# A hybrid decoder layer with sparse experts: one-hots of a gate table built eight tokens at a time, gather steps and last chunks in another order

## The chip, the cores and the metric

The kernel runs on one core of one Trainium2 chip. The metric is the device time of one execution in microseconds (us); of several runs the median is taken. The profile is of one further execution, with its own time.

## The reference, cut to what matters

The layer is attention and a gated recurrence side by side, then PEER: each of 512 tokens picks, for each of 8 heads, 16 of 16384 experts, and an expert is one row of `u` and one row of `v` (1024 numbers each). `h` is the normalised token, `idx` the 128 experts of a token, `gates` their softmax weights.

```python
def expert_block(args):
    ht, it, gt = args
    ue = jnp.take(u, it, axis=0)
    act = jax.nn.gelu(jnp.einsum('tkd,td->tk', ue, ht), approximate=False)
    ve = jnp.take(v, it, axis=0)
    return jnp.einsum('tk,tkd->td', gt * act, ve)
...
x = x + peer_layer(rms_norm(x, norm_ffn_g), w_peer_q, peer_keys, peer_u, peer_v)
...
return rms_norm(x, norm_final_g)
```

An expert's number is i1*128 + i2, from two lists of 128 keys. The inputs are float32.

## The kernel before, in words

**Two ways through the experts.** The first 160 tokens are done as the reference does them. 320 steps each fetch one expert row per partition by an indirect DMA (`gather`, L704, issued on POOL at L707, 512 KB, into one of four buffers `ga`), and then VectorE (DVE) uses the 128 rows: `sparse` (L711) multiplies them with `h` and sums (L715) or adds them, weighted, to the sum (L725). `pace(goal, after)` (L729) brings the number of gathers issued up to `goal`; behind each it records the DVE step of the gather three places earlier (`GLAG`), and that step may not stand on its engine ahead of the instruction `after`.

The other 352 tokens meet all experts as dense matrices. `u` comes in 128 chunks of 128 experts, each loaded by SP (L152), split into a high part `hi` by ScalarE (ACT, L142) and a rest `lo` by DVE (L162), and put through 24 matmuls (`act_pieces`, L638, matmuls L646: 16 with `hi`, then 8 with `lo`); ACT's Gelu (L652) leaves a tile `gel`. Three raw buffers (`S4`) and two each of `hi` and `lo` (`HB`) are turned over. Chunks of `v` are handled in the main loop.

**The gate table.** A gate of a token belongs to an expert (i1, i2). For each token TensorE multiplies a one-hot of i2 over the 128 picks by a one-hot of i1 that carries the gates, high and low part (two matmuls 128x128 in f16, L912). VectorE makes the one-hots for eight tokens at a time (`oh`, two buffers) by four operations, L904 to L907; `iok` is a table of the numbers 0 to 127, repeated. ACT copies four tokens' results from PSUM into `G` (L914), and each 16 tokens a DMA on ACT's queue stores `G` to the DRAM tensor `Gd` (L916): 22 steps. Between the one-hot matmuls `piece` (L672) feeds six matmuls of a U chunk at a time, 88 pieces in all, the matmuls kept in program order (`keep_in_program_order`). `pace((s_ + 1) // 3, ...)` sets gathers beside the table.

**Behind the table.** 26 U chunks are done ahead of the table and 22 in it; five more are held back (`HELD`): three by `fill` (L662) at once and two (`LASTU`) behind `g_load(0)`, which reads the first gates back from `Gd` (L936) and so waits for the last store. `pace(EARLY, ...)` brings the gathers to 16. In the text A is the chunk in work as the table ends, B, C, D the next three, E and F the last two.

**The main loop.** For each of 128 chunks of `v`: split (L142, L162), `w` = gel * gates (L980, waits for `gt`), its split (L142, L985), then 18 matmuls 128x512 (L994 to L996) into six PSUM banks `acc`; then U chunks still to do, then `pace` in proportion, with all gathers issued `TAILC` = 2 chunks before the end. The last two chunks (`TL`) go together. Behind the loop stand the last gather steps and `final_rows` (L960 add, L967 scale, store).

Within an engine a scheduler puts instructions in the order of the program unless an instruction's inputs are late by its reckoning; `tc.issue_after(x)` makes what is recorded under it stand behind `x` on their engine. Each queue (SP, ACT, POOL) issues its DMAs in order.

Of the kernel before, what the change touches and what calls it, by code (L numbers as in the profile page):

```python
# [17 lines left out]
P = 128  # L18
# [8 lines left out]
NE = 128  # L27
# [10 lines left out]
GS = 4096.0  # L38
GC = 4
TG = 16  # L40
QT = 4
OT = 8
LOOK = 26
LATE = 17
S4 = 3
# [1 line left out]
VPRE = 2  # L47
GLAG = 3
GB = 4
TAILC = 2  # L50
HELD = 5
LASTU = 2
EARLY = 16
# [63 lines left out]
def layer(nc, tc, a, out, probe=None, upto=99):  # L117
# [5 lines left out]
    cur = {}  # L123
# [31 lines left out]
    def wsplit(raw, shape, parts=1, eng=None):  # L155
        hi = oc.tile(list(shape), F32R, tag="hi", bufs=HB, name=nm("hi"))
        lo = oc.tile(list(shape), F32R, tag="lo", bufs=HB, name=nm("lo"))
        n = shape[1] // parts
        for i in range(parts):
            m = slice(i * n, (i + 1) * n)  # L160
            hi_of(hi[:, m], raw[:, m])
            (eng or V).tensor_tensor(lo[:, m], raw[:, m], hi[:, m].bitcast(F32), op=OP.subtract)  # L162
        return hi, lo


# [26 lines left out]
    with tc.tile_pool(name="front", bufs=1) as fr, tc.tile_pool(name="psf", bufs=1, space=PSUM) as psf:  # L192
# [79 lines left out]


        ktm, logf = [], []
        POOL.dma_start(gm, a["gmix"])
        POOL.dma_start(ones, a["const"][:, 5 * P:6 * P])
        ld = exp_ln_set()
        fb = proj_tm(0)
# [342 lines left out]
    with tc.tile_pool(name="peer", bufs=1) as pp, tc.tile_pool(name="psp", bufs=1, space=PSUM) as psp, ExitStack() as ps:  # L621
# [45 lines left out]
                    nu[0] += 1  # L667


        work = []  # L670

        def piece(limit):  # L672
            while len(work) < 2 and nu[0] < limit:
                work.append(act_pieces(next(todo), True))
                next(work[-1])
                nu[0] += 1
            if work and next(work[0], 0) == 0:
                work.pop(0)

        gta = pp.tile([P, NB, PH * TK], F32, name="gta")  # L680
# [195 lines left out]
        with tc.tile_pool(name="gb", bufs=1, reuse_waits="tile") as gp:  # L876
            iT = gp.tile([P, 2, DT], F16, name="iT")
            gs = gp.tile([P, DT], F32, name="gs")
            g16 = gp.tile([P, 2, DT], F16, name="g16")
            fill(2)  # L880
            for n in range(1, NB):
                f = X if n == 1 else 0
                t = slice((n - 1) * P - X + f, n * P - X)
                b = bank((P, 4, P))
                for w in range(2):
                    PE.transpose(b[:, w, :], i12[:, w, n, :], ident)
                PE.transpose(b[:, 2, :], gta[:, n, :], ident)
                ACT.activation(iT[:, :, t], b[:, 0:2, f:], AF.Copy)
                ACT.activation(gs[:, t], b[:, 2, f:], AF.Copy, scale=GS)  # L889
                V.tensor_copy(g16[:, 0, t], gs[:, t])  # L890
                V.tensor_tensor(g16[:, 1, t], gs[:, t], g16[:, 0, t], op=OP.subtract)
            NQ = OT // QT
            shape = [P, NQ, P, QT]
            for s_ in range(NPT):
                G_ = gp.tile([P, NE, TG], F32, tag="G", bufs=2, name=nm("G"))
                for o in range(TG // OT):
                    t = slice(s_ * TG + o * OT, s_ * TG + (o + 1) * OT)

                    def row(x):
                        return x.rearrange("p (q t) -> p q t", t=QT).unsqueeze(2).to_broadcast(shape)  # L900

                    ioq = iok.unsqueeze(1).to_broadcast(shape)
                    oh = gp.tile([P, 3, NQ, P, QT], F16, tag="oh", bufs=2, name=nm("oh"))
                    V.tensor_tensor(oh[:, 0], ioq, row(iT[:, 0, t]), op=OP.is_equal)  # L904
                    V.tensor_tensor(oh[:, 2], ioq, row(iT[:, 1, t]), op=OP.is_equal)
                    V.tensor_tensor(oh[:, 1], oh[:, 2], row(g16[:, 0, t]), op=OP.mult)
                    last = V.tensor_tensor(oh[:, 2], oh[:, 2], row(g16[:, 1, t]), op=OP.mult)  # L907
                    for q in range(NQ):
                        b = bank((P, QT, P))
                        for i in range(QT):  # L910
                            for w in range(2):
                                lastg = tc.keep_in_program_order(PE.matmul(b[:, i, :], oh[:, 0, q, :, i], oh[:, 1 + w, q, :, i], start=w == 0, stop=w == 1))  # L912
                        m = o * OT + q * QT
                        ACT.activation(G_[:, :, m:m + QT].rearrange("p c t -> p t c"), b, AF.Copy)  # L914
                        piece(KEEP - HELD)
                ACT.dma_start(Gd.rearrange("g p s f -> s p g f")[s_], G_.rearrange("p (g c) t -> p g (c t)", c=GC))  # L916
                pace((s_ + 1) // 3, last.ins)
        late = ps.enter_context(tc.tile_pool(name="late", bufs=1, reuse_waits="tile"))
        cur["late"] = late

# [12 lines left out]
        def g_load(g):  # L933
            if g < NE // GC:
                gts[g] = late.tile([P, NPT, GC * TG], F32, tag="gt", bufs=2, name=nm("gt"))
                return SP.dma_start(gts[g], Gd[g])  # L936

        with tc.issue_after(lastg.ins):
            fill(KEEP - nu[0] - LASTU)
        for c in range(VPRE):  # L940
            v_load(c)
        g0 = g_load(0)
        pace(EARLY, last.ins)
        with tc.issue_after(lastg.ins), tc.issue_after(g0.ins):
            fill(LASTU)

# [26 lines left out]
        for c in range(NE):  # L973
            if c % GC == 0:
                g_load(c // GC + 1)
            gtile = gts[c // GC][:, :, (c % GC) * TG:(c % GC + 1) * TG]
            v_load(c + VPRE)
            vh, vl = wsplit(vraw.pop(c), [P, D])
            w = late.tile([P, DT], F32, tag="w", bufs=2, name=nm("w"))
            V.scalar_tensor_tensor(w.rearrange("p (s t) -> p s t", t=TG), gel.pop(c).rearrange("p (s t) -> p s t", t=TG),  # L980
                                   1.0 / GS, gtile, op0=OP.mult, op1=OP.mult)
            whi = late.tile([P, DT], F32R, tag="whi", bufs=2, name=nm("whi"))
            hi_of(whi, w)
            wlo = late.tile([P, DT], F32R, tag="wlo", bufs=2, name=nm("wlo"))
            last = V.tensor_tensor(wlo, w, whi.bitcast(F32), op=OP.subtract)  # L985
            ready.append((c, whi, wlo, vh, vl))
            if c < NE - TL or c == NE - 1:
                for tb in range(DB):
                    t = slice(tb * P, min(tb * P + P, DT))
                    m = t.stop - t.start  # L990
                    for i, whi, wlo, vh, vl in ready:
                        for hf in range(2):
                            d = slice(hf * 512, (hf + 1) * 512)
                            PE.matmul(acc[tb][hf][0:m, :], whi[:, t], vh[:, d], start=i == 0, stop=False)  # L994
                            PE.matmul(acc[tb][hf][0:m, :], whi[:, t], vl[:, d], start=False, stop=False)  # L995
                            PE.matmul(acc[tb][hf][0:m, :], wlo[:, t], vh[:, d], start=False, stop=i == NE - 1)  # L996
# [24 lines left out]
            pace(EARLY + (NS - EARLY) * share, last.ins)  # L1021

        while nsp[0] < NS:
            sparse(nsp[0])
            nsp[0] += 1
        final_rows(ys[0], [sp0.ax[:, 0:512], sp0.ax[:, 512:]], 0, P)
        for n in range(DB):
            m = min(P, DT - n * P)
            final_rows(ys[n + 1][0:m, :], [acc[n][hf][0:m, :] for hf in range(2)], T0 + n * P, m)
# [17 lines left out]
```

## Time and profile before

| what | us |
|---|---|
| three runs: median (lowest to highest) | 1666.84 (1663.52 to 1667.65) |
| the profiled execution, its own time | 1675.46 |
| its span | 1673.7 |
| TensorE (PE) busy | 1605.2 (96 %) |
| VectorE (DVE) busy | 1321.9 (79 %) |
| ScalarE (ACT) busy | 709.6 (42 %) |
| GpSimd (POOL) busy | 487.3 (29 %) |
| mean granted TensorE clock | 0.986 of full |

The span is what the trace covers; the execution's own time is 1.8 us longer. In the timelines a row of several equal instructions gives the start of the first and the length from there to the end of the last; TensorE's matmuls overlap their neighbours, so the step from one start to the next, not the length, is what one costs. A wait is the idle time of an engine, with the instruction or the transfer that ended it.

### The profile page before, as it was taken

The numbers are of one execution on the slowest core, as the hardware profiler recorded it, in microseconds if no ns is written. First come the engines' busy times: TensorE is split into PE (matmuls) and PEld (weight loads), VectorE is DVE, ScalarE is ACT, GpSimd is POOL, SyncE is SP. The second block draws the span as 40 slices with busy tenths as digits, with TensorE's granted clock in tenths as the row PEclk, the third lists the DMA queues.
The fourth block names the chain that finished last, engine by engine and source line by source line (L and its number), as shares of the span: only waits on it lengthen the run. The fifth ranks groups of instructions, "written<-read, shape, count | busy, mean of one in ns | idle before, by whom it ended". The sixth has DMA issues, their size and how long they took to land.

```text
span 1673.7 us, 23435 instructions
## 1 busy us (share of the span) xinstructions
PE 1605.2 (96%) x8511; PEld 1358.7 (81%) x8511; DVE 1321.9 (79%) x2560; ACT 709.6 (42%) x1152; POOL 487.3 (29%) x341
## 2 busy tenths in 40 slices
PE   8999999999999969997899999999999999999996
PEld 6877678888988869997788888887888888888874
DVE  8456663647999988887688888878888888888887
ACT  5433353234554547775333333333333333333333
POOL 4000000000000010002455555445455555554542
PEclk9999999999999979999899999999999999999998
DMA  5311133334333347888999999999999999999984
GB/s 173 101 51 51 51 104 111 103 115 154 108 109 116 103 126 192 219 224 265 336 340 353 349 368 349 337 341 339 344 368 351 359 354 347 360 358 363 343 305 145
DMA packets 197491, 400.87 MB, mean 240 GB/s; under 512 B 103344, under 2 KB 105904, under 8 KB 197376
## 3 DMA queue, kind: packets, MB, share of 16 engines
q1 hardware_dynamic: 58832, 206.02, 35.2%
q0 software_dynamic: 46336, 168.39, 27.0%
q10 hardware_dynamic: 92208, 24.98, 6.1%
q8 instruction: 66, 1.08, 0.3%
q14 instruction: 49, 0.40, 0.1%
HBM read 371.91 MB, written 27.39 MB: 239 GB/s over the span
## 4 chain that ended last, share of the span: by engine, by line
PE 53%; issue 16%; POOL 12%; DVE 12%; DMA 6%; ACT 1%; POOLq 0%; DVEq 0%; SPq 0%; ACTq 0%
PE b L646 13%; POOL ga L707 11%; PE b L263 5%; PE b L262 5%; PE b L995 5%; PE b L996 5%; PE b L265 4%; PE b L994 4%; DMA ga<-v,idx 4%; PE b L912 4%; DVE lo L162 3%; DMA ga<-un,idx 1%; DVE ti L858 1%; DVE mr L856 1%; DVE e L725 1%
## 5 line engine op out<-in xcount | busy, mean ns | idle before, releaser
L707 POOL DMA_INDIRECT ga<-un,idx x160 | 225.2, 1407 | 944.5 <-ACT gs L889 581.3
L646 PE MATMUL b<-hT,hi 128*128 128x352 f32 x2048 | 366.9, 327 | 2.2 <-ACT hi L142 1.7
L646 PEld LDWEIGHTS b<-hT,hi 128*128 128x128 f32 x2048 | 334.4, 190 | 12.7 <-ACT hi L142 2.0
L995 PE MATMUL b<-lo,whi 128*128 128x512 f32 (+1 forms) x768 | 305.0, 397 | 15.0 <-DVE lo L162 14.6
L996 PE MATMUL b<-hi,wlo 128*128 128x512 f32 (+1 forms) x768 | 304.3, 396 | 0.0
L994 PE MATMUL b<-hi,whi 128*128 128x512 f32 (+1 forms) x768 | 302.7, 395 | 0.0
L707 POOL DMA_INDIRECT ga<-v,idx x160 | 240.4, 1502 | 208.3 <-DVE e L725 190.3
L142 ACT ACTIVATE hi<-s 128x1024 fp32r<-128x1024 f32 (+1 forms) x195 | 205.1, 1052 | 203.1 <-PE b L646 88.1
L162 DVE TENSOR_TENSOR lo<-s,hi 128x1024 fp32r<-128x1024 f32 (+1 forms) x195 | 238.5, 1224 | 29.7 <-ACT hi L142 28.0
L142 ACT ACTIVATE whi<-w 128x352 fp32r<-128x352 f32 x128 | 63.7, 498 | 400.0 <-PE b L995 361.2
L725 DVE SCALAR_TENSOR_TENSOR e<-ga,wt,e 128x1024 f32<-128x1024 f32 x158 | 202.2, 1280 | 19.3 <-DMA ga<-v,idx 18.4
L715 DVE SCALAR_TENSOR_TENSOR ga<-ga,h 128x1024 f32<-128x1024 f32 x160 | 194.5, 1220 | 28.6 <-DMA ga<-un,idx 26.9
L646 PE MATMUL b<-hT,lo 128*128 128x352 f32 x1024 | 191.3, 325 | 11.8 <-DVE lo L162 11.8
L995 PEld LDWEIGHTS b<-lo,whi 128*128 128x128 f32 (+1 forms) x768 | 138.8, 181 | 59.2 <-DVE lo L162 22.0
L646 PEld LDWEIGHTS b<-hT,lo 128*128 128x128 f32 x1024 | 168.0, 189 | 12.4 <-DVE lo L162 12.3
L996 PEld LDWEIGHTS b<-hi,wlo 128*128 128x128 f32 (+1 forms) x768 | 138.5, 180 | 39.3
L994 PEld LDWEIGHTS b<-hi,whi 128*128 128x128 f32 (+1 forms) x768 | 138.2, 180 | 35.3 <-ACT hi L142 1.2
L142 ACT ACTIVATE hi<-vr 128x1024 fp32r<-128x1024 f32 x128 | 134.6, 1051 | 75.9 <-PE b L646 46.3
L162 DVE TENSOR_TENSOR lo<-vr,hi 128x1024 fp32r<-128x1024 f32 x128 | 156.1, 1220 | 9.4 <-ACT hi L142 9.4
L263 PE MATMUL b<-hT,hi 128*128 128x512 f32 (+1 forms) x376 | 146.4, 391 | 0.3 <-DVE hT L145 0.3
L262 PE MATMUL b<-hT,hi 128*128 128x512 f32 (+1 forms) x376 | 146.1, 390 | 0.2
L985 DVE TENSOR_TENSOR wlo<-w,whi 128x352 fp32r<-128x352 f32 x128 | 67.0, 523 | 80.9 <-ACT whi L142 77.5
(284 smaller groups left out, 1960.5 us busy)
## 6 DMA issues: line engine op xcount, KB each, us to landing
s<-uc SPq DMA_DIRECT2D x128, 512.0 KB
vr<-vc SPq DMA_DIRECT2D x128, 512.0 KB
Gd<-G ACTq DMA_DIRECT2D x22, 1024.0 KB
gt<-Gd SPq DMA_DIRECT2D x32, 704.0 KB
s<-wfm SPq DMA_DIRECT2D x30, 512.0 KB
s<-wq SPq DMA_DIRECT2D x16, 512.0 KB
s<-wmg SPq DMA_DIRECT2D x8, 512.0 KB
s<-wout SPq DMA_DIRECT2D x8, 512.0 KB
```

The lines of the kernel that those rows point to most:

```text
L142: ACT.activation(dst, src, AF.Copy)
L162: (eng or V).tensor_tensor(lo[:, m], raw[:, m], hi[:, m].bitcast(F32), op=OP.subtract)
L262: PE.matmul(b, wh[:, k, :], rh(i), start=start and i == 0, stop=False)
L263: PE.matmul(b, wh[:, k, :], rl(i), start=False, stop=False)
L646: m = PE.matmul(o, w[:, k, :], z[:, k, t], start=i == 0, stop=i == 3 * KD - 1)
L707: tc.keep_in_program_order(POOL.indirect_dma_start(out=t, out_offset=None, in_=a[src], in_offset=bass.IndirectOffsetOnAxis(ap=b.idx[:, j:j ...
L715: V.scalar_tensor_tensor(t, t, 1.0, h20, op0=OP.mult, op1=OP.mult, accum_out=b.act[:, j:j + 1])
L725: V.scalar_tensor_tensor(b.ax, t, b.wt[:, j:j + 1], b.ax, op0=OP.mult, op1=OP.add)
L985: last = V.tensor_tensor(wlo, w, whi.bitcast(F32), op=OP.subtract)
L994: PE.matmul(acc[tb][hf][0:m, :], whi[:, t], vh[:, d], start=i == 0, stop=False)
L995: PE.matmul(acc[tb][hf][0:m, :], whi[:, t], vl[:, d], start=False, stop=False)
L996: PE.matmul(acc[tb][hf][0:m, :], wlo[:, t], vh[:, d], start=False, stop=i == NE - 1)
```

## The change

1. The one-hots of eight tokens are made by two DVE operations of 128x2048 in place of four of 128x1024. The layout of `oh` changes with it: a token's 128 values stand eight f16 apart (16 bytes) where they stood four apart (8 bytes); `iok` has 1024 entries in place of 512. The number and the order of the matmuls and of ACT's copies stay.
2. `piece` takes a second limit: loads and splits of two more U chunks are begun within the table, their matmuls left for after it. Each of the three chunks behind the table is followed by one gather, whose DVE step stands behind that chunk's `lo`; `pace(EARLY, ...)` goes behind the last of these.
3. Beside the table `pace` asks for a gather every two steps, 11 by its end, in place of 7.
4. `TAILC` is 5; the last gather steps and the first 128 tokens' `final_rows` stand in chunk 125 of the loop; the matmuls of the last two chunks run through the bank's halves ahead of the chunks.
5. `gm`, a load at the program's start, moves from POOL's queue to ACT's.

```diff
-QT = 4
-OT = 8
+QT = 8
+BT = 4
-TAILC = 2
+TAILC = 5
...
-        POOL.dma_start(gm, a["gmix"])
+        ACT.dma_start(gm, a["gmix"])
...
-        def piece(limit):
-            while len(work) < 2 and nu[0] < limit:
-                work.append(act_pieces(next(todo), True))
-                next(work[-1])
+        def piece(limit, ahead):
+            while len(work) < 2 and nu[0] < ahead:
+                c = next(todo)
+                work.append((c, act_pieces(c, True)))
+                next(work[-1][1])
                 nu[0] += 1
-            if work and next(work[0], 0) == 0:
+            if work and work[0][0] < limit and next(work[0][1], 0) == 0:
                 work.pop(0)
...
-                    oh = gp.tile([P, 3, NQ, P, QT], F16, tag="oh", bufs=2, name=nm("oh"))
-                    V.tensor_tensor(oh[:, 0], ioq, row(iT[:, 0, t]), op=OP.is_equal)
-                    V.tensor_tensor(oh[:, 2], ioq, row(iT[:, 1, t]), op=OP.is_equal)
-                    V.tensor_tensor(oh[:, 1], oh[:, 2], row(g16[:, 0, t]), op=OP.mult)
-                    last = V.tensor_tensor(oh[:, 2], oh[:, 2], row(g16[:, 1, t]), op=OP.mult)
+                    oh = gp.tile([P, 3, P, QT], F16, tag="oh", bufs=2, name=nm("oh"))
+                    V.tensor_tensor(oh[:, 1:3], ioq, iT[:, :, t].unsqueeze(2).to_broadcast(shape), op=OP.is_equal)
+                    last = V.tensor_tensor(oh[:, 0:2], oh[:, 1:2].to_broadcast(shape),
+                                           g16[:, :, t].unsqueeze(2).to_broadcast(shape), op=OP.mult)
...
-                                lastg = tc.keep_in_program_order(PE.matmul(b[:, i, :], oh[:, 0, q, :, i], oh[:, 1 + w, q, :, i], start=w == 0, stop=w == 1))
+                                lastg = tc.keep_in_program_order(PE.matmul(
+                                    b[:, i, :], oh[:, 2, :, q * BT + i], oh[:, 1 - w, :, q * BT + i],
+                                    start=w == 0, stop=w == 1))
...
-                        piece(KEEP - HELD)
+                        piece(KEEP - HELD, KEEP - HELD + 2)
...
-                pace((s_ + 1) // 3, last.ins)
+                pace((s_ + 1) // 2, last.ins)
...
+        held = cur["lo"]
+        for c_, g_ in work:
+            for _ in g_:
+                pass
+            pace(nga[0] + 1, held.ins)
         with tc.issue_after(lastg.ins):
-            fill(KEEP - nu[0] - LASTU)
+            for _ in range(KEEP - nu[0] - LASTU):
+                fill(1)
+                held = cur["lo"]
+                pace(nga[0] + 1, held.ins)
...
-        pace(EARLY, last.ins)
+        pace(EARLY, held.ins)
...
-                    for i, whi, wlo, vh, vl in ready:
-                        for hf in range(2):
-                            d = slice(hf * 512, (hf + 1) * 512)
+                    for hf in range(2):
+                        d = slice(hf * 512, (hf + 1) * 512)
+                        for i, whi, wlo, vh, vl in ready:
...
-        while nsp[0] < NS:
-            sparse(nsp[0])
-            nsp[0] += 1
-        final_rows(ys[0], [sp0.ax[:, 0:512], sp0.ax[:, 512:]], 0, P)
+            if c == NE - 3:
+                while nsp[0] < NS:
+                    sparse(nsp[0])
+                    nsp[0] += 1
+                final_rows(ys[0], [sp0.ax[:, 0:512], sp0.ax[:, 512:]], 0, P)
```

The order of VectorE behind the table, before: the last one-hots (`oh`), then gather steps (`ga`, L715) and the `lo` parts of U chunks (L162), then the first `w`, which waits for the gates `gt`.

```order
L907 TENSOR_TENSOR oh_7456<-oh_7456,g_5521 128x1024
L715 SCALAR_TENSOR_TENSOR ga_6902,act_3079<-ga_6902,h_62 128x1024
L715 SCALAR_TENSOR_TENSOR ga_7159,act_3079<-ga_7159,h_62 128x1024
L715 SCALAR_TENSOR_TENSOR ga_7414,act_3079<-ga_7414,h_62 128x1024
L162 TENSOR_TENSOR lo_7349<-s_1252_7346,hi_7348 128x1024
L715 SCALAR_TENSOR_TENSOR ga_7609,act_3079<-ga_7609,h_62 128x1024
L715 SCALAR_TENSOR_TENSOR ga_7612,act_3079<-ga_7612,h_62 128x1024
L715 SCALAR_TENSOR_TENSOR ga_7615,act_3079<-ga_7615,h_62 128x1024
L715 SCALAR_TENSOR_TENSOR ga_7618,act_3079<-ga_7618,h_62 128x1024
L715 SCALAR_TENSOR_TENSOR ga_7621,act_3079<-ga_7621,h_62 128x1024
L715 SCALAR_TENSOR_TENSOR ga_7624,act_3079<-ga_7624,h_62 128x1024
L162 TENSOR_TENSOR lo_7510<-s_1275_7507,hi_7509 128x1024
```

And now (the same lines are L903, L717 and L162):

```order
L903 TENSOR_TENSOR oh_7385<-oh_7385,g_5521 128x2048
L717 SCALAR_TENSOR_TENSOR ga_6932,act_3079<-ga_6932,h_62 128x1024
L162 TENSOR_TENSOR lo_7279<-s_1256_7276,hi_7278 128x1024
L162 TENSOR_TENSOR lo_7359<-s_1267_7356,hi_7358 128x1024
L717 SCALAR_TENSOR_TENSOR ga_7096,act_3079<-ga_7096,h_62 128x1024
L162 TENSOR_TENSOR lo_7469<-s_1284_7466,hi_7468 128x1024
L717 SCALAR_TENSOR_TENSOR ga_7259,act_3079<-ga_7259,h_62 128x1024
L162 TENSOR_TENSOR lo_7504<-s_1289_7501,hi_7503 128x1024
L717 SCALAR_TENSOR_TENSOR ga_7422,act_3079<-ga_7422,h_62 128x1024
L717 SCALAR_TENSOR_TENSOR ga_7463,act_3079<-ga_7463,h_62 128x1024
L717 SCALAR_TENSOR_TENSOR ga_7498,act_3079<-ga_7498,h_62 128x1024
L988 SCALAR_TENSOR_TENSOR w_7620<-gel_3136,gt_7540 128x352
```

Between the last one-hots and the `lo` of chunk B stood nine gather steps and now stands one; the `lo` of C and D have one more each ahead of them, and three gather steps stand between D's `lo` and the first `w`.

VectorE in the tail of the changed kernel, from the last but one gather step (L727) on; `lo_14811` is the split of `v` chunk 124, `lo_14841` that of chunk 125:

```order
L727 SCALAR_TENSOR_TENSOR e_528_3077<-ga_14723,wt_3080,e_528_3077 128x1024
L727 SCALAR_TENSOR_TENSOR e_528_3077<-ga_14775,wt_3080,e_528_3077 128x1024
L968 TENSOR_TENSOR s_2731_14681<-s_2731_14681,b_14756 32x512
L968 TENSOR_TENSOR s_2731_14681<-s_2731_14681,b_14758 32x512
L162 TENSOR_TENSOR lo_14811<-vr_14726,hi_14810 128x1024
...
L968 TENSOR_TENSOR e_2729_14678<-e_2729_14678,e_528_3077 128x512
L162 TENSOR_TENSOR lo_14841<-vr_14778,hi_14840 128x1024
```

Before, the last gather step stood between the `lo` of chunk 126 and that of chunk 127, and the adds of the first 128 tokens behind both. Now it stands ahead of the `lo` of chunk 124.

## Rows read from the trace of the kernel before

**Rows 1.** Stretches: us; busy PE, PEld, DVE, ACT, POOL; granted clock, DMA share, GB/s

```profile
621.00:783.00 162.00, 160.72 (x1171) 148.68 (x1170) 140.10 (x200) 114.08 (x124) 10.40 (x7) 1.00 0.79 213
783.00:802.00 19.00, 6.53 (x34) 5.95 (x33) 8.44 (x13) 4.49 (x5) 8.53 (x7) 0.79 1.02 341
...
819.00:1640.00 821.00, 810.05 (x4039) 686.65 (x4039) 697.16 (x893) 297.07 (x408) 427.72 (x304) 1.00 0.95 348
1640.00:1674.00 34.00, 19.07 (x71) 13.66 (x69) 22.23 (x34) 10.73 (x29) 9.70 (x1) 0.81 0.34 115
```

**Rows 2.** Waits of PE, 819 to 1640: us in total, times, longest

```profile
PE b L995 <- DVE lo L162: 10.5, 12, 3.2
```

**Rows 3.** PE timeline, end of table: start us, length us, [idle before <-releaser]

```profile
775.31 1.11 PE L912 MATMUL b<-oh 128*128 128x128 f16 x8
776.17 1.22 PE L646 MATMUL b<-hT,hi 128*128 128x352 f32 x6
777.23 1.11 PE L912 MATMUL b<-oh 128*128 128x128 f16 x8
...
781.92 0.59 PE L646 MATMUL b<-hT,lo 128*128 128x352 f32 x2 [1.01 <-DVE lo L162]
...
799.72 2.71 PE L646 MATMUL b<-hT,lo 128*128 128x352 f32 x8 [10.75 <-DVE lo L162]
802.23 3.71 PE L646 MATMUL b<-hT,hi 128*128 128x352 f32 x16
...
818.82 0.40 PE L994 MATMUL b<-hi,whi 128*128 128x512 f32 x1
```

**Rows 4.** Waits of DVE, 775 to 805, as rows 2

```profile
DVE ga L715 <- DMA ga<-un,idx: 9.2, 4, 3.7
```

**Rows 5.** DVE timeline behind the table, as rows 3

```profile
798.44 2.35 DVE L162 TENSOR_TENSOR lo<-s,hi 128x1024 fp32r<-128x1024 f32 x2
...
808.26 0.96 DVE L980 SCALAR_TENSOR_TENSOR w<-gel,gt 128x352 f32<-128x352 f32 x2 [4.51 <-DMA gt<-Gd]
```

**Rows 6.** Waits of the queue of SP, 775 to 830, as rows 2

```profile
SPq L936 <- DMA Gd<-G: 20.4, 1, 20.4
```

**Rows 7.** ACT timeline behind the table, as rows 3

```profile
810.00 1.05 ACT L142 ACTIVATE hi<-s 128x1024 fp32r<-128x1024 f32 x1
```

**Rows 8.** Gathers (L707) from 1600 on: duration ns min/median/max, first and last start

```profile
L707 POOL DMA_INDIRECT ga<-v,idx x13: 936/1674/9908, 1600.6 to 1639.8; - x13
```

**Rows 9.** DVE timeline in the tail, as rows 3

```profile
1653.36 1.28 DVE L725 SCALAR_TENSOR_TENSOR e<-ga,wt,e 128x1024 f32<-128x1024 f32 x1 [4.48 <-DMA ga<-v,idx]
...
1663.06 2.73 DVE L967 SCALAR_TENSOR_TENSOR e<-e,rs,h 128x512 f32<-128x512 f32 x4
```

**Rows 10.** PE timeline in the tail, as rows 3

```profile
1655.84 0.80 PE L995 MATMUL b<-lo,whi 128*128 128x512 f32 x1 [4.04 <-DVE lo L162]
...
1662.71 0.40 PE L996 MATMUL b<-hi,wlo 128*96 128x512 f32 x1
```

**Rows 11.** Timeline of all engines at the start, as rows 3

```profile
5.31 0.72 ACT L216 ACTIVATE hT<-s,gm 128x512 fp32r<-128x512 f32 x1 [3.29 <-DMA gm<-gmix]
```

**Rows 12.** DVE groups by form: out<-in, shapes, count, busy us, mean ns, idle

```profile
L904 DVE TENSOR_TENSOR oh<-iok,iT 128x1024 f16<-128x1024 f16 x44 | 30.4, 691 | 23.1 <-PE b L912 22.2 <-ACT iT L888 0.8
...
L816 DVE TENSOR_TENSOR eq<-iota,r 128x2048 f16<-128x2048 f16 x8 | 9.8, 1224 | 0.7
```

**Rows 13.** PE groups by form, as rows 12

```profile
L646 PE MATMUL b<-hT,hi 128*128 128x352 f32 x2048 | 366.9, 327 | 2.2 <-ACT hi L142 1.7 <-ACT s L613 0.5
...
L912 PE MATMUL b<-oh 128*128 128x128 f16 x704 | 98.2, 296 | 3.2 <-DVE oh L906 2.0 <-DVE oh L907 1.2
...
L262 PE MATMUL b<-hT,hi 128*128 128x256 f32 x16 | 4.1, 294 | 0.1
```

**Rows 14.** ACT groups by form, as rows 12

```profile
L914 ACT ACTIVATE G<-b 128x512 f32<-128x512 f32 x88 | 96.0, 1091 | 54.3 <-PE b L912 50.7 <-issue 3.7
...
L844 ACT ACTIVATE qp<-b 128x512 f32<-128x512 f32 x15 | 9.0, 600 | 4.0 <-PE b L265 4.0
```

More of the change, by code (lines that the diff above doesn't have):

```diff
@@ L161, in wsplit @@
             hi_of(hi[:, m], raw[:, m])
-            (eng or V).tensor_tensor(lo[:, m], raw[:, m], hi[:, m].bitcast(F32), op=OP.subtract)
+            cur["lo"] = (eng or V).tensor_tensor(lo[:, m], raw[:, m], hi[:, m].bitcast(F32), op=OP.subtract)
         return hi, lo
@@ L885, in layer @@
                 for w in range(2):
-                    PE.transpose(b[:, w, :], i12[:, w, n, :], ident)
+                    PE.transpose(b[:, w, :], i12[:, 1 - w, n, :], ident)
                 PE.transpose(b[:, 2, :], gta[:, n, :], ident)
@@ L889, in layer @@
                 ACT.activation(gs[:, t], b[:, 2, f:], AF.Copy, scale=GS)
[L890 to L893, printed above, removed]
+                V.tensor_copy(g16[:, 1, t], gs[:, t])
+                V.tensor_tensor(g16[:, 0, t], gs[:, t], g16[:, 1, t], op=OP.subtract)
+            shape = [P, 2, P, QT]
+            ioq = iok.unsqueeze(1).to_broadcast(shape)
@@ L894, in layer @@
             for s_ in range(NPT):
                 G_ = gp.tile([P, NE, TG], F32, tag="G", bufs=2, name=nm("G"))
[L896 to L902, printed above, removed]
-                    oh = gp.tile([P, 3, NQ, P, QT], F16, tag="oh", bufs=2, name=nm("oh"))
-                    V.tensor_tensor(oh[:, 0], ioq, row(iT[:, 0, t]), op=OP.is_equal)
-                    V.tensor_tensor(oh[:, 2], ioq, row(iT[:, 1, t]), op=OP.is_equal)
-                    V.tensor_tensor(oh[:, 1], oh[:, 2], row(g16[:, 0, t]), op=OP.mult)
-                    last = V.tensor_tensor(oh[:, 2], oh[:, 2], row(g16[:, 1, t]), op=OP.mult)
-                    for q in range(NQ):
-                        b = bank((P, QT, P))
-                        for i in range(QT):
-                            for w in range(2):
-                                lastg = tc.keep_in_program_order(PE.matmul(b[:, i, :], oh[:, 0, q, :, i], oh[:, 1 + w, q, :, i], start=w == 0, stop=w == 1))
-                        m = o * OT + q * QT
-                        ACT.activation(G_[:, :, m:m + QT].rearrange("p c t -> p t c"), b, AF.Copy)
-                        piece(KEEP - HELD)
@@ new lines, in layer @@
+                for o in range(TG // QT):
+                    t = slice(s_ * TG + o * QT, s_ * TG + (o + 1) * QT)
+                    oh = gp.tile([P, 3, P, QT], F16, tag="oh", bufs=2, name=nm("oh"))
+                    V.tensor_tensor(oh[:, 1:3], ioq, iT[:, :, t].unsqueeze(2).to_broadcast(shape), op=OP.is_equal)
+                    last = V.tensor_tensor(oh[:, 0:2], oh[:, 1:2].to_broadcast(shape),
+                                           g16[:, :, t].unsqueeze(2).to_broadcast(shape), op=OP.mult)
+                    for q in range(QT // BT):
+                        b = bank((P, BT, P))
+                        for i in range(BT):
+                            for w in range(2):
+                                lastg = tc.keep_in_program_order(PE.matmul(
+                                    b[:, i, :], oh[:, 2, :, q * BT + i], oh[:, 1 - w, :, q * BT + i],
+                                    start=w == 0, stop=w == 1))
+                        m = o * QT + q * BT
+                        ACT.activation(G_[:, :, m:m + BT].rearrange("p c t -> p t c"), b, AF.Copy)
+                        piece(KEEP - HELD, KEEP - HELD + 2)
```

## The prediction

> **What bounds the kernel now.** I read first the table of stretches [rows 1]. While the gate table is built (621 to 783) TensorE is busy 160.72 of 162 us and VectorE 140.10: TensorE sets the pace. In the main loop it is busy 810.05 of 821 us, and of its waits there the view of waits names 10.5 us, for VectorE's `lo` [rows 2]. Two stretches are not full: 783 to 802, with 6.53 us of work in 19, and the tail from 1640, with 19.07 in 34. Only there can an order give much; in the other two only a dearer or cheaper matmul counts.
>
> Then the timeline of TensorE at the table's end [rows 3]. It stalls 1.01 us before 781.92 and 10.75 us before 799.72, both times for a `lo`. After the long stall it is slow as well: eight matmuls take 799.72 to 802.23, 2.51 us, where six took 777.23 less 776.17, 1.06, so eight should take 1.41; the next sixteen cover 3.71 us. The granted clock, full in the table, was 0.79 of full over that stretch [rows 1]. I put the slow matmuls at 2 us.
>
> Why the `lo` is late: VectorE waits 9.2 us in four gather steps, the longest 3.7 [rows 4], and makes the two `lo` only from 798.44 on [rows 5]. The order printed above says why: nine gather steps stand between the last one-hots and the second `lo`. But a second chain ends late too. SP's queue waits 20.4 us for the last store of the table before it may issue the load of the gates [rows 6]; VectorE's first `w` starts at 808.26, ended by that load [rows 5]; ACT splits chunk E only at 810.00, behind the two splits of `w` [rows 7]; so the main loop opens at 818.82 [rows 3].
>
> In the tail the last gather takes 9.91 us on POOL, the median of 13 being 1.674 [rows 8]. VectorE waits 4.48 us for it, until 1653.36 [rows 9], and TensorE 4.04 us behind that, until 1655.84; its last matmul starts at 1662.71 [rows 10]. From 1663.06 four operations of 2.73 us, of rows long complete, stand on VectorE ahead of the last add [rows 9].
>
> **The change, part by part.**
>
> *Behind the table.* The `lo` of A, B, C and D now have one gather step or none ahead of each. The stall of 1.01 goes. TensorE then has A's rest and B, C, D, three chunks of 24 matmuls at 1.06/6 = 0.177, 4.2 us each: work until about 797. What is late next is the gates. The store is in line with gathers: before, six steps were free to run at once, now each of three waits for a `lo`, so about three gathers of 512 KB less are ahead of or beside it. At 341 GB/s [rows 1] that is 4.6 us, and with the 1.01 us of the earlier table end the load of the gates goes some 5.6 us sooner. E, F and the main loop follow at the same distances, so the loop opens about 812.8 in place of 818.82: **-6**. Ends: -1 if the store lands when it did (only the first stall goes, and the waiting moves from B's `lo` to E's `hi`); -14 if all goes, 1.01 + 10.75 + 2. I take -6, nearest to the chain of the gates, which the change does not shorten otherwise.
>
> *One-hots on VectorE.* Four operations of 0.69 us become two of 128x2048 f16, whose nearest row is the comparison L816, 1.224 us [rows 12]. Per eight tokens 4 x 0.69 - 2 x 1.22 = 0.32 us, by 44: 14 us less of VectorE. It buys no time: before the first of the four operations VectorE is idle 22.2 us, waiting for TensorE's one-hot matmuls [rows 12]. The four more gather steps (1.23 each) and two more splits in the table, some 7 us, fit into it. DMA: four gathers and two chunks are 3 MB, beside 213 GB/s x 162 us = 34.5 MB at a share of 0.79 [rows 1]: to about 0.86. **0**, covered by TensorE's work; without the cover it would be the 14 us.
>
> *One-hots on TensorE.* 704 matmuls stay, but read both operands at steps of 16 bytes, not 8. Eight cost 776.17 less 775.31 = 0.86 us, 0.108 each [rows 3]. No row has the new step. Ends: 0 (a wider step does not make reads cheaper) and a doubling, 0.108 x 704 = +76, all of it on the path. For the low end: a matmul L912 of 128 columns lasts 296 ns, L262 with 256 packed ones 294 [rows 13], and by 0.177 us for 352 columns [rows 3] 128 packed ones would cost 0.064; the present step is already dearer by 1.7. The nearest row for a wide step is ACT's copy L914, which writes four bytes in every 64: 1091 ns where the packed copy L844 takes 600 [rows 14], a factor of 1.8. So a wide step costs about what the 8-byte step costs now, and I take **0**.
>
> The Trainium skill speaks against this part: its page "SBUF — State Buffer", section "Specifications (TRN2)", says that full bandwidth needs two hits or more in each 16-byte line. Step 8 has two hits, step 16 one, so by it the sum would be up to 76 us worse. The trace only half agrees: with two hits per line the reads are not at full rate here, as far as L912 shows.
>
> *The main loop.* Ending five chunks early in place of two packs the gathers into 198 parts where they had 201 (`pace` divides by 128 and the 75 U chunks left, less TAILC): 1.5 % more steps per chunk. VectorE is busy 697.16 of 821 there [rows 1], so most is hidden; what it waits on it shares with `lo`, 10.5 us [rows 2]. Ends 0 and +5 (1.5 % of the 304 steps at 1.25 us), I take **+1**, since VectorE is full only in some of the chunks.
>
> *The tail.* The last gather is still the last instruction of POOL's queue but three chunks earlier, and its step is now ahead of chunk 124's `lo`. Whatever made it slow is not touched, so I expect the stall of some 4 us to move there, with its slow clock. Gained: the last add no longer stands behind 2.73 us of others [rows 9]. Given back: between the stall and the last `lo` VectorE has about 13 us of splits, `w` and adds, about as much as TensorE has matmuls for, so a microsecond or two of new waiting. **-1.5**; ends +2 (all given back) and -7 (the gather comes in time: 4.04 and some 2.5 of slow clock).
>
> *The start.* ACT waits 3.29 us for `gm` until 5.31, behind which the first matmul stands [rows 11]. Issued on ACT's queue rather than as POOL's first transfer it should land sooner: **-1**, ends 0 and -1.4.
>
> Sum: -6 + 0 + 0 + 1 - 1.5 - 1 = **-7.5**. On the profiled execution's 1675.46 that is 1668.0; it stands 8.6 above the median of the three runs, and on the median, 1666.84, it is **1659**.
>
> **The rivals.**
>
> *B, the gates hide it.* If the store lands when it did, and the last gather is slow again: -1 + 1 - 0.5 - 1 = -1.5, **1665**. For it: the 20.4 us of SP's queue [rows 6] are longer than the stall that goes, and DMA is at 1.02 in that stretch [rows 1]. Against it: fewer gathers beside the store.
>
> *C, the wide step halves TensorE's reads.* A new line of memory for each element, 0.216 per matmul: +76 in the table, the rest as forecast: 1659 + 76 = **1735**. It decides from about +0.011 us per matmul on (7.5/704), where the gain is used up. For it: L912's present price need not be the step's; weights of 128 columns are loaded for each matmul as well. Against it: L914's factor at 64 bytes. It is what the rule on lines in the Trainium skill's page "SBUF — State Buffer", section "Specifications (TRN2)", would do at its worst.
>
> *D, part of that.* If a quarter is added, 0.027 x 704 = +19: **1678**.
>
> *E, both stalls vanish.* -14 behind the table, -7 in the tail, -1 at the start, +1: -21, **1646**. It needs the gates early and the last gather quick.
>
> **How the numbers follow.** About 0.3 % (5 us) is what a measurement of this kernel can tell from no change. Chances: forecast 0.52, B 0.17, C 0.14, D 0.10, E 0.07. Faster by over 0.3 %, below 1661.8: most of the forecast's case (0.45), a little of B (0.04) and E: 0.56. Within: the rest of these two, 0.20. Slower: C and D, 0.24. The range 1648 to 1684 takes the forecast's ends, B, D and half of E and leaves C out. The likeliest case by itself spans 1652 to 1665.
>
> **What would show it.** Right: the step of eight one-hot matmuls still 0.86 us; no stall of TensorE above 4 us between the table's end and the first main-loop matmul, that one some 6 us sooner against the table's end; the gates' load still the last to end a wait there; the last gather again near 10 us, with TensorE's stall at chunk 124 and the last add right behind the last matmul. Wrong: eight one-hot matmuls at 1.7 us (C); a stall of the old length at another place (B); no slow gather (E); VectorE waits in the main loop well above 10.5 us.

## The result and the profile after

The changed kernel takes 1814.36 us (median of six, 1812.87 to 1819.78), the kernel before on the same chip 1663.47: a ratio of 1.0899, with a 95 % interval of 1.0879 to 1.0919. It is 151 us slower where 7.5 us faster was forecast.

The stretches of the changed kernel (length; busy time of PE, PEld, DVE, ACT, POOL with counts; granted clock, DMA share, GB/s), the answer to [rows 1]:

```profile
608.00:927.00 319.00, 318.90 (x1229) 245.42 (x1229) 139.75 (x127) 122.14 (x130) 17.21 (x12) 0.50 0.44 127
927.00:957.00 30.00, 23.62 (x125) 22.74 (x125) 18.17 (x27) 9.74 (x14) 10.14 (x9) 0.90 0.81 281
957.00:1770.00 813.00, 792.56 (x3976) 675.39 (x3975) 687.50 (x878) 289.79 (x394) 428.84 (x302) 1.00 0.94 348
```

The loss is in the first line. The table takes 319 us, TensorE is busy throughout, and the granted clock is 0.50 of full, the lower of its two levels, from the first one-hot to the last. In the timeline of TensorE inside the table both kinds of matmul are dear:

```profile
622.59 2.07 PE L909 MATMUL b<-oh 128*128 128x128 f16 x8
624.30 2.12 PE L646 MATMUL b<-hT,hi 128*128 128x352 f32 x6
626.23 2.08 PE L909 MATMUL b<-oh 128*128 128x128 f16 x8
```

Eight one-hot matmuls step from 622.59 to 624.30, 1.71 us, 0.214 each, and six of a U chunk to 626.23, 1.93 us, 0.32 each; before it was 0.108 and 0.177 [rows 3]. VectorE did get cheaper, as the group of the comparisons shows, but only waits longer for TensorE (last column):

```profile
L902 DVE TENSOR_TENSOR oh<-iok,iT 128x2048 f16<-128x2048 f16 x44 | 53.9, 1225 | 170.3 <-PE b L909 169.4
```

Single rows of the changed trace that answer to [rows 11], [rows 6], [rows 2] and [rows 8], in that order: the start, the wait for the table's last store, TensorE's waits in the main loop (957 to 1778), the gathers from 1700 on:

```profile
3.89 0.72 ACT L216 ACTIVATE hT<-s,gm 128x512 fp32r<-128x512 f32 x1 [1.41 <-DMA gm<-gmix]
```

```profile
SPq L935 <- DMA Gd<-G: 13.4, 1, 13.4
```

```profile
PE b L1003 <- DVE lo L162: 20.4, 13, 2.7
```

```profile
L709 POOL DMA_INDIRECT ga<-v,idx x26: 939/1676/2115, 1699.2 to 1771.7; - x26
```

`gm` lands 1.4 us sooner; the store is waited for 7 us less; the main loop waits twice as long for `lo`; and no gather is slow, the longest takes 2.115 us.

Stage by stage, from the timelines of TensorE of the profiled executions, this one and those of the experiments (us):

| kernel | table: first to last one-hot | to the main loop | main loop | its last matmul to the end |
|---|---|---|---|---|
| before | 171.97 | 35.35 | 844.29 | 10.54 |
| changed | 318.51 | 30.40 | 845.75 | 8.35 |
| e2_onehot | 318.51 | 29.58 | 837.57 | 10.54 |
| e3_warm | 251.53 | 30.18 | 850.03 | 8.36 |
| e1_rest | 169.63 | 33.47 | 847.15 | 8.36 |
| e1_tailc2 | 170.48 | 32.43 | 837.17 | 10.17 |
| e4_pace | 170.87 | 36.43 | 836.53 | 10.18 |
| q2 | 149.15 | 33.13 | 844.61 | 8.35 |
| q2_best | 151.42 | 35.70 | 832.91 | 10.19 |
| q2_oldpace | 151.09 | 36.08 | 834.86 | 10.17 |
| q2_pace3 | 146.74 | 31.69 | 838.87 | 10.16 |
| w8_m16 | 246.78 | 29.30 | 842.19 | 8.36 |
| w16_m8 | 173.66 | 32.50 | 846.46 | 8.35 |
| step32 | 400.92 | 28.79 | 843.19 | 8.35 |

Before's main loop has 4.04 us of stall [rows 10] and some 2.5 us of low clock in it from the one slow gather [rows 8] (its matmuls behind the stall take 6.87 us, the same ones in e2_onehot 4.36); without them it would be some 838, an estimate.

### The profile page after: what moved, and what is told of

Its sections match the earlier page's. It is cut to its first block, busy times and chain, and to the rows that moved or that the text cites. A ratio compares the mean times of both kernels' runs of the same rounds, so it can differ in the third digit from the quotient of the medians.

```text
span 1811.1 us, 23343 instructions
## 1 busy us (share of the span) xinstructions
PE 1751.4 (97%) x8511; PEld 1447.0 (80%) x8511; DVE 1314.1 (73%) x2472; ACT 712.1 (39%) x1152; POOL 479.8 (26%) x340
## 4 chain that ended last, share of the span: by engine, by line
PE 60%; DVE 14%; issue 10%; DMA 7%; POOL 7%; ACT 1%; POOLq 0%; DVEq 0%; SPq 0%; ACTq 0%
PE b L646 17%; PE b L909 9%; POOL ga L709 7%; PE b L1003 5%; PE b L1004 5%; PE b L1002 5%; DMA ga<-v,idx 5%; PE b L263 4%; PE b L262 4%; PE b L265 4%; DVE lo L162 4%; DMA ga<-un,idx 1%; DVE e L727 1%; DVE ti L860 1%; DVE mr L858 1%
## 5 line engine op out<-in xcount | busy, mean ns | idle before, releaser
L646 PE MATMUL b<-hT,hi 128*128 128x352 f32 x2048 | 421.3, 359 | 3.8 <-ACT hi L142 3.3
L646 PEld LDWEIGHTS b<-hT,hi 128*128 128x128 f32 x2048 | 378.1, 212 | 20.2 <-ACT hi L142 3.9
L709 POOL DMA_INDIRECT ga<-v,idx x160 | 233.1, 1457 | 205.4 <-DVE e L727 187.8
L162 DVE TENSOR_TENSOR lo<-s,hi 128x1024 fp32r<-128x1024 f32 (+1 forms) x195 | 239.4, 1228 | 43.7 <-ACT hi L142 42.0
L646 PE MATMUL b<-hT,lo 128*128 128x352 f32 x1024 | 218.4, 357 | 3.1 <-DVE lo L162 3.1
L727 DVE SCALAR_TENSOR_TENSOR e<-ga,wt,e 128x1024 f32<-128x1024 f32 x158 | 202.1, 1279 | 18.7 <-DMA ga<-v,idx 17.9
L717 DVE SCALAR_TENSOR_TENSOR ga<-ga,h 128x1024 f32<-128x1024 f32 x160 | 194.3, 1220 | 26.0 <-DMA ga<-un,idx 22.4
L646 PEld LDWEIGHTS b<-hT,lo 128*128 128x128 f32 x1024 | 190.9, 212 | 5.3 <-DVE lo L162 3.4
L1003 PEld LDWEIGHTS b<-lo,whi 128*128 128x128 f32 (+1 forms) x768 | 138.1, 180 | 62.8 <-DVE lo L162 25.9
L909 PE MATMUL b<-oh 128*128 128x128 f16 x704 | 182.6, 417 | 2.3 <-DVE oh L903 2.3
L902 DVE TENSOR_TENSOR oh<-iok,iT 128x2048 f16<-128x2048 f16 x44 | 53.9, 1225 | 170.3 <-PE b L909 169.4
L913 ACT ACTIVATE G<-b 128x512 f32<-128x512 f32 x88 | 94.9, 1078 | 184.2 <-PE b L909 184.2
L162 DVE TENSOR_TENSOR lo<-vr,hi 128x1024 fp32r<-128x1024 f32 x128 | 156.0, 1219 | 7.1 <-ACT hi L142 6.6
```

The lines of the kernel that those rows point to most:

```text
L162: cur["lo"] = (eng or V).tensor_tensor(lo[:, m], raw[:, m], hi[:, m].bitcast(F32), op=OP.subtract)
L646: m = PE.matmul(o, w[:, k, :], z[:, k, t], start=i == 0, stop=i == 3 * KD - 1)
L709: tc.keep_in_program_order(POOL.indirect_dma_start(out=t, out_offset=None, in_=a[src], in_offset=bass.IndirectOffsetOnAxis(ap=b.idx[:, j:j ...
L717: V.scalar_tensor_tensor(t, t, 1.0, h20, op0=OP.mult, op1=OP.mult, accum_out=b.act[:, j:j + 1])
L727: V.scalar_tensor_tensor(b.ax, t, b.wt[:, j:j + 1], b.ax, op0=OP.mult, op1=OP.add)
L913: ACT.activation(G_[:, :, m:m + BT].rearrange("p c t -> p t c"), b, AF.Copy)
```

## The experiments

**e1_rest: the change without its one-hots.** The layout and the four operations of before, in the changed kernel:

```diff
-QT = 8
+QT = 4
+OT = 8
...
-                    oh = gp.tile([P, 3, P, QT], F16, ...)
+                    oh = gp.tile([P, 3, NQ, P, QT], F16, ...)
```

> The changed kernel with the one-hots of before (four operations, step 8 bytes), all else of the change kept. Theory 1, the 16-byte step is the whole loss and the rest is worth what was forecast for it: the one-hots back at 0.108 us, granted clock 1.00 in the table, 1663.5 - 7.5 = 1656, between 1652 and 1661. Rival, the rest of the change (two more chunks and four more gathers beside the table) keeps the clock down: one-hots at 0.108 but U matmuls at 0.32 us, 528 x 0.145 = 76 us more, about 1735.

Measured: 1671.88 against 1667.8 before, ratio 1.0024 (1.0008 to 1.0041), clock 0.988. The table is back at 169.63 us, so the one-hots are the whole loss; but the rest is 4 us slower, not 7.5 faster. The theory is right on the first half, wrong on the second. The rival falls.

**e2_onehot: the kernel before with the new one-hots alone.** The two operations and the `oh` of the change's diff, nothing else of it.

> The kernel before with only the new one-hots (two operations, step 16 bytes). Theory 1: the loss of the changed kernel is here, 0.107 us on 704 one-hot matmuls and 0.145 us on 528 U matmuls in the table, 75 + 76 = 151, without the gain of the rest: 1663.5 + 151 = 1815 to 1822. Rival, the clock stays down only because of the other parts: 1663.5 + 75 = 1739.

One run gives 1806.86, 139 us above before and 8 under what was expected, its table 318.51 us and at the low clock, as in the changed kernel:

```profile
608.00:927.00 319.00, 318.11 (x1226) 244.49 (x1225) 139.42 (x126) 121.01 (x128) 16.37 (x12) 0.50 0.43 121
```

The 75 us of the rival are excluded: the one-hots alone keep the clock down. Against its own kernel before it loses 12 us less than the whole change; e1_rest puts 4 of them down to the rest of the change. Its tail is that of before, and its last gathers take 2.114 us at most: the 9.91 us of [rows 8] did not come back.

**e3_warm: the changed kernel entered at full clock.**

```diff
-            fill(2)
             for n in range(1, NB):
...
+            with tc.issue_after(lastt.ins):
+                fill(2)
             shape = [P, 2, P, QT]
```

> The changed kernel with the two U chunks that stand ahead of the table moved between its transposes and its first one-hot, so that TensorE works without a pause, at full clock, up to the table. They then start some 8 us later than before. Theory 1, one-hot reads at 0.215 us leave TensorE's matmuls waiting so much that the clock falls from full as well: granted clock 0.50 in most of the table, 1814 + 8 = 1822, 1812 to 1830. Rival, the clock only never rises because the table is entered at the low level: it stays at 1.00, one-hots 0.215 and U matmuls 0.177, 1814 - 76 + 8 = 1746.

Measured, in one run: 1753.59, clock 0.989 over the span. My own theory fell; the rival, with 1746, holds. The stretches just ahead of the table and of the table, and the timeline inside it:

```profile
603.00:612.00 9.00, 9.00 (x52) 8.81 (x51) 6.35 (x12) 4.84 (x9) 5.11 (x4) 0.92 0.68 209
612.00:863.00 251.00, 251.00 (x1227) 186.85 (x1225) 138.23 (x124) 119.67 (x130) 14.37 (x9) 1.00 0.54 153
```

```profile
683.45 2.07 PE L910 MATMUL b<-oh 128*128 128x128 f16 x8
685.15 1.32 PE L646 MATMUL b<-hT,hi 128*128 128x352 f32 x6
686.31 2.07 PE L910 MATMUL b<-oh 128*128 128x128 f16 x8
```

At full clock a one-hot still takes 1.70/8 = 0.2125 us, a U matmul 1.16/6 = 0.193 in place of 0.32. So the 146.5 us of the table have two parts: 251.53 - 171.97 = 80 for the reads at full clock, and 318.51 - 251.53 = 67 for a clock that never rose. Of the first part 704 x (0.2125 - 0.108) = 74 us are the one-hots themselves; the U matmuls among them, at 0.193 where they took 0.177, add some 8 (why, no run shows), 82 together, as against e1_rest's 169.63.

In these two runs the clock stayed through the whole table at the level at which it was entered. In the kernel before the table is entered low too, after TensorE's idle 11.4 us for the top-k, but there the clock rises some 5 us behind the first one-hot (611.50), as two stretches and the timeline show: six U matmuls in 1.91 us, then in 1.21. With the 16-byte one-hots alone (e2_onehot) it did not rise in 319 us. What in them keeps it down is not shown.

```profile
612.00:616.00 4.00, 3.30 (x19) 3.04 (x19) 2.63 (x5) 1.08 (x1) 1.79 (x2) 0.50 0.94 313
617.00:621.00 4.00, 4.00 (x31) 3.71 (x30) 2.68 (x5) 3.02 (x4) 0.00 (x0) 1.00 0.22 88
```

```profile
613.44 2.11 PE L646 MATMUL b<-hT,hi 128*128 128x352 f32 x6
615.35 1.14 PE L912 MATMUL b<-oh 128*128 128x128 f16 x8
616.24 1.37 PE L646 MATMUL b<-hT,hi 128*128 128x352 f32 x6
617.45 1.11 PE L912 MATMUL b<-oh 128*128 128x128 f16 x8
```

At a step of 16 bytes the price of a one-hot does not depend on the clock, 0.214 us low and 0.2125 full: it is the read. At 8 bytes eight take 0.89 us low and 0.86 full, which says less: by the 1.91 us of six U matmuls of 352 columns, 128 packed columns would cost some 0.116 at the low level as well, an estimate.

**q2: a step of 4 bytes.** e1_rest with two tokens side by side, `QT = 2` in place of 4.

> As e1_rest, with the one-hots of two tokens side by side: step 4 bytes in place of 8, still four operations of 1024 elements. Theory L, a read pays for each 16-byte line it touches (0.215 at one value per line, 0.107 at two): at four per line the one-hot matmul costs the 0.064 us of packed columns, 0.043 x 704 = 30 us less of TensorE in the table; VectorE, some 133 us busy there, then comes near to the bound, so 15 to 30 us under e1_rest, if its operations stay at 0.69 us. Rival, 0.107 us is a floor of these small matmuls (weight load and stream) and not of the step: the same as e1_rest within 5 us.

Measured: 1650.49, ratio 0.9918 (0.9887 to 0.9949), 21 us under e1_rest.

```profile
648.39 0.63 PE L916 MATMUL b<-oh 128*128 128x128 f16 x8
648.83 1.24 PE L647 MATMUL b<-hT,hi 128*128 128x352 f32 x6
```

Eight in 0.44 us, 0.055 each, where theory L had 0.064. It holds; the 0.107 us was no floor. By the steps 4, 8 and 16 bytes a matmul of 128 columns costs 0.055, 0.108 and 0.2125 us. VectorE's operations stay at 0.69 us, and it is nearly full in the table now: 143.8 us busy of 149, TensorE waiting 10.1 us for one-hots.

**w8_m16 and w16_m8: which operand.** Both in e3_warm, with a separate tile for the weights:

```diff
-                                    b[:, i, :], oh[:, 2, :, q * BT + i], oh[:, 1 - w, :, q * BT + i],
+                                    b[:, i, :], ow[:, q, :, i], oh[:, 1 - w, :, q * BT + i],
```

(in w16_m8 `ow[:, :, q * BT + i]` at step 16 and `oh[:, 1 - w, q, :, i]` at step 8).

> As e3_warm (table entered at full clock, both operands at step 16 there, 0.215 us a matmul), but the operand that is loaded as weights lies at step 8 bytes; the one that streams stays at 16. Theory M, the stream's reads set the price: still 0.215, about 1754. Theory W, the weight load's reads set it: 0.108, 75 us less, about 1679. If each adds half: 0.16, about 1716.

> The other way round: weights at step 16 bytes, the streamed operand at 8, one VectorE operation more. Theory M: 0.108, about 1679. Theory W: 0.215, about 1754. Each adds half: 0.16, about 1716. If whichever is slower sets it, this one and the one before both stay at 1754.

Measured, in one run each: 1740.38 and 1675.34. The timeline of w8_m16, then of w16_m8:

```profile
682.31 2.01 PE L918 MATMUL b<-oh,ow 128*128 128x128 f16 x8
683.96 1.32 PE L646 MATMUL b<-hT,hi 128*128 128x352 f32 x6
```

```profile
680.33 1.17 PE L918 MATMUL b<-oh,ow 128*128 128x128 f16 x8
681.25 0.89 PE L646 MATMUL b<-hT,hi 128*128 128x352 f32 x4
```

1.65/8 = 0.206 with only the streamed operand at 16 bytes, 0.92/8 = 0.115 with only the weights there. Theory M: the stream sets the price, the weights add 0.007. That w8_m16 is 13 us under e3_warm is by 5 us the table; 8 us are its main loop, 842 us long, where the other runs with a `TAILC` of 5 have 843 to 850.

**e1_tailc2: the gathers end at the old place.** e1_rest with `TAILC = 2`.

> e1_rest with TAILC back at 2, the tail's code as in the change. Theory T, ending the gathers five chunks early packs VectorE fuller and costs the main loop the 7 to 9 us more of waits for lo that the runs with TAILC 5 show (17 to 20 us, where those with 2 have 10 to 11): waits back near 10.5, 5 to 8 us under e1_rest, about 1665. Rival, the waits come from another order of gather steps and splits that is fixed at the table's end: no change, 1672.

Measured: 1660.51, ratio 0.9948 (0.9929 to 0.9968), 11 us under e1_rest. TensorE's waits in the main loop, of e1_rest and then of e1_tailc2:

```profile
PE b L1010 <- DVE lo L163: 17.0, 16, 3.1
```

```profile
PE b L1010 <- DVE lo L163: 8.1, 10, 3.2
```

The main loop takes 837.17 us in place of 847.15, the end 10.17 in place of 8.36: theory T, and more than its 5 to 8 us. In the table above the seven main loops with TAILC 5 (changed, e1_rest, e3_warm, q2, w8_m16, w16_m8, step32) last 842 to 850 us, the others, but for before with its slow gather, 833 to 839.

Why 1.5 % costs so much is shown in part. By the formula of `pace` gathers come whole: worked out for all 128 chunks, a chunk with a U chunk to do gets three gather steps, and with a divisor of 201 four of them in chunks 0, 72 and 97; with 198 in chunks 0, 17, 34, 51, 60, 68, 77, 85, 94, 102 and 111. In e1_rest TensorE's waits of 0.4 us and more begin, among others, in chunks 18, 35, 52, 78, 86, 95, 103 and 112: one behind eight of these. They make up 8.1 of the 17.0 us; behind the fourth steps of e1_tailc2 there are 1.1. Six more waits of e1_rest, with the longest, stand behind no fourth step. It isn't that VectorE has no time left: in the 16 us ahead of each of the eight it is idle itself, for the transfer of a gather, as here ahead of the wait in chunk 35.

```profile
1043.22 1.22 DVE L718 SCALAR_TENSOR_TENSOR ga<-ga,h 128x1024 f32<-128x1024 f32 x1 [1.83 <-DMA ga<-un,idx]
```

```profile
1049.88 0.50 PE L1010 MATMUL b<-lo,whi 128*128 128x512 f32 x1 [1.14 <-DVE lo L163]
```

So the gathers of a fuller chunk seem to come late, with the DMA engines busy for 0.94 of the loop. No run tests this by itself.

**e4_pace: the old order beside and behind the table.** e1_tailc2 with `piece` and `pace` of before; `gm` and the tail stay as changed.

> e1_tailc2 with the order beside and behind the table as before the change: no chunks begun ahead, a gather every three steps, nine gather steps ahead of the second lo. What is left of the change is the load of gm and the tail. Theory P, the pacing part is worth what the stages show (171.97 + 35.35 us from the first one-hot to the main loop before, 170.48 + 32.43 now): 4.4 us slower than e1_tailc2, about 1665. Rival, those stages differ by chance and the gain lies elsewhere: 1660.5 within 2 us.

Measured: 1665.56, ratio 0.9979 (0.9960 to 0.9998), 5 us above e1_tailc2, but against a kernel before at 1669.32 where that one had 1667.61; by the ratios they are 0.3 % apart, and the two intervals just touch. SP's queue waits for the last store, in e4_pace and in e1_tailc2:

```profile
SPq L942 <- DMA Gd<-G: 21.0, 1, 21.0
```

```profile
SPq L942 <- DMA Gd<-G: 11.7, 1, 11.7
```

The stage to the main loop is 36.43 against 32.43 us: theory P. TensorE's longest stall there, in e4_pace (with the row of E's first matmuls) and then in e1_tailc2, and VectorE's wait ahead of the first `w` in e1_tailc2:

```profile
797.96 2.71 PE L647 MATMUL b<-hT,lo 128*128 128x352 f32 x8 [9.84 <-DVE lo L163]
...
809.76 2.81 PE L647 MATMUL b<-hT,hi 128*128 128x352 f32 x16 [0.89 <-ACT hi L143]
```

```profile
803.80 4.63 PE L647 MATMUL b<-hT,hi 128*128 128x352 f32 x16 [8.76 <-ACT hi L143]
```

```profile
800.10 0.96 DVE L995 SCALAR_TENSOR_TENSOR w<-gel,gt 128x352 f32<-128x352 f32 x2 [6.01 <-DMA gt<-Gd]
```

The stall moved from B's `lo` to E's `hi`, which stands behind the split of the first `w`, and that waits for the gates. This `w` starts 19.2 us behind the end of the table in place of 25.9, 6.7 us sooner, but only 4 of these reach the main loop: E's first sixteen matmuls take 4.63 us behind the stall, at a granted clock of 0.50 (798 to 807), and 2.81 us in e4_pace, at full.

**q2_best, q2_oldpace, q2_pace3: a version that beats both.** q2 with `TAILC = 2` and one comparison of 128x2048 for two of 128x1024 (the lists of i1 and i2 laid out by eights, so that four dimensions do); then the old order of e4_pace, or `pace((s_ + 1) // 3, ...)` alone.

> q2 (step 4 bytes) with TAILC 2 and the two comparisons of eight tokens in one VectorE operation of 128x2048, the products still two. If VectorE bounds q2's table (143.8 busy of 149, TensorE waiting 10.1 us for one-hots) the 0.15 us less per eight tokens, 6.6 us in all, shortens it by most of that, and if theory T holds the loop gives 5 to 8 more: 1650.5 - 5 - 6 = 1640. If neither: 1650.

> q2_best with the order beside and behind the table as before the change. Its table is now short of DMA (share 0.94, TensorE waits 12.3 us for splits of late chunks), and this takes four gathers and two chunks, 3 MB, out of it: at 252 GB/s up to 12 us of the table. Theory D, DMA bounds that table: the table shorter by 5 to 10 us, but the nine gather steps behind it stall the lo again: 1639.5 plus or minus 4. If DMA does not bound it: 4 us slower, 1643.

> q2_best with a gather every three steps of the table in place of two (7 in it, not 11), the chunks begun ahead and the order behind the table kept. Theory D: 2 MB less beside the table, its waits for hi shrink by some 6 us, of which the gathers behind it take back half: about 1636. Rival, VectorE alone bounds the table: 1639.5 or a little less, four steps of 1.23 us moved out and back in.

Measured, in this order: 1639.45, 1642.61 and 1634.86; ratios 0.9824 (0.9803 to 0.9845), 0.9837 (0.9804 to 0.9870) and 0.9785 (0.9755 to 0.9816). q2_best came out at its number for another reason: the loop gave 11.7 us, the table none (151.42 after 149.15). What ACT waits for in its table, 610 to 756, shows the next bound, and so does TensorE:

```profile
ACT G L922 <- DMA Gd<-G: 34.1, 11, 6.0
```

```profile
PE b L647 <- ACT hi L143: 12.3, 9, 3.8
```

ACT waits for the stores of `G`, of which there are two buffers, and the splits of U chunks queue behind it. With four gathers fewer beside the table both shrink, to 27.8 and 5.2 us in q2_pace3, and the table to 146.74, as theory D has it. q2_oldpace speaks against it: with the same four gathers and two chunks fewer TensorE's waits for `hi` shrink as much, to 5.4 us, but its table stays at 151.09, where theory D had 5 to 10 us less; its total lies in the range of either theory. There the waits for `lo`, none in q2_best, are 4.0 us. So what bounds this table is open. The best version, q2_pace3, is 2.15 % faster than the kernel before.

**step32: a step of 32 bytes.** e3_warm with half of `oh` left unused and one buffer of it.

> As e3_warm with the one-hots 32 bytes apart (half of the places unused) and one buffer of them in place of two, so VectorE and TensorE take turns and the time as a whole tells nothing. Only the step of a one-hot matmul is read. Theory L, a streamed read pays for each 16-byte line: one value a line at 16 and at 32 bytes, so 0.2125 us again. Rival, the price grows with the step: 0.42 us.

```profile
697.08 2.12 PE L910 MATMUL b<-oh 128*128 128x128 f16 x8
698.84 2.12 PE L646 MATMUL b<-hT,lo 128*128 128x352 f32 x6
```

1.76/8 = 0.22 us, as at 16 bytes at either clock: the price stops growing at one value per line. This run shows one thing more. Its table is entered at full clock, as in e3_warm, but with one buffer TensorE waits 71.6 us in it for one-hots, and at 622 the clock falls and stays low to the table's end:

```profile
612.00:621.00 9.00, 7.39 (x36) 5.30 (x36) 3.68 (x3) 2.69 (x4) 0.00 (x0) 1.00 0.38 144
622.00:1012.00 390.00, 320.05 (x1186) 239.11 (x1186) 137.06 (x123) 123.33 (x128) 8.43 (x9) 0.50 0.35 98
```

## Why the prediction was wrong

*One-hots on TensorE, the step that failed.* The prediction took 0 between 0 and +76, by the "nearest row for a wide step", the ACT copy L914. The runs show +80 for the reads, 74 of it in the one-hots themselves, and +67 more for a clock that they kept low. L914 is a write by another engine; it says nothing on TensorE's stream. The other argument, that "the present step is already dearer by 1.7", was right (2.0, by q2's 0.055) but was read the wrong way: a price that had nearly doubled against packed columns was a sign that it follows the step, and would double again. The rule of the Trainium skill's page "SBUF — State Buffer", section "Specifications (TRN2)", pointed the right way. The measured price is harsher than that rule: two hits per line stream at half the rate of four, 0.108 us against 0.055, and these four cost no more per column than the packed U matmuls (0.177 us for 352, 0.064 for 128).

*Rival C* had the mechanism, at 0.14, and half the size: it gave 1735. What it missed is the clock, 67 us: I took "full in the table" as given, though the same trace shows the table entered at 0.50 and the clock rising only behind its first pieces. With the 16-byte one-hots among them these pieces did not lift it. The range, 1648 to 1684, left C out.

*Behind the table: -6.* Right in mechanism and nearly in size: 4 us in the stage by e4_pace and e1_tailc2, 5 by the medians; the store is waited for 9 us less, and with the old one-hots the gates still end last, as said. The sign "no stall of TensorE above 4 us" did not come with the old one-hots, 8.76 us stand ahead of E, and it did not fit the prediction's own times: work until 797 and a loop that opens at 812.8 with E and F ahead of it leave some 7 us idle. In the changed kernel itself the gates are there before the first `w`, and no stall is over 3.1 us.

*The main loop: +1, ends 0 and +5.* Wrong in size: +8 to +10 (the changed kernel against e2_onehot, e1_rest against e1_tailc2), beyond the end. The mean over the loop hid it; the steps fall whole on single chunks, four in one chunk three times before and eleven times now.

*The tail: -1.5.* The end after the last matmul is 2.2 us shorter with TAILC 5, as argued from [rows 9], 0.4 with TAILC 2. But the slow gather did not move to chunk 124; it did not come back in any of the 13 other traces, where the longest is 2.50 us. It belongs to that one execution, what made it is open, and it explains some 6.5 of the 12 us by which that execution stood above the later median. I built rival E and a term on a single instance.

*The start: -1.* Right: first matmul at 5.80 in place of 6.61. *One-hots on VectorE: 0.* Right in the changed kernel, at 1.225 us for an operation as its row had it; the cover was TensorE, in a table twice as long. No run has the two operations at the old step.

With its one-hots at the old step, as in e1_rest, the change comes out about even, stage by stage: -0.8 at the start, (169.63 + 33.47) - (171.97 + 35.35) = -4.2 in the table and behind it, +9 in the main loop and -2.2 at the end, together about +2; 4 were measured.

## What to carry to other kernels

When a layout makes one engine's operations fewer, price the other engine's reads of it: TensorE's streamed operand wants its values packed in a 16-byte line, and here that was worth more than VectorE's savings. Count discrete work per loop turn, not its mean, where a loop is nearly full. And look at the clock where a stage begins: a change that makes matmuls dearer or lets them wait can cost the clock on top of its own price, as it did here and in step32. A row that shows something once in an execution is no term of a sum.

## What the runs showed of the hardware

A streamed f16 operand of 128 columns cost 0.055, 0.108, 0.2125 and 0.22 us at steps of 4, 8, 16 and 32 bytes: from 8 bytes on about 1.7 ns for each 16-byte line touched (0.108 us over 64 lines, 0.2125 over 128), and at 16 bytes the same at both clock levels (0.214 and 0.2125). Weights at 16 bytes added only 0.007. And in one and the same mix of matmuls the granted clock stayed at 0.50 for 319 us where the table was entered low, behind an idle TensorE, and at 1.00 for 251 us where it was entered at full, behind matmuls without a pause (603 to 612 in e3_warm); in step32, with waits among them, it fell from full.
